# A hybrid encoder block on one core: gate row moved into gate/up, down-phase buffers and queue order rearranged

## The chip, the cores and the metric

One core of one Trainium2 chip runs the whole layer. The metric is the device time of one execution in microseconds (us); lower is better. TensorE (PE) does the matrix products, VectorE (DVE) and ScalarE (ACT) the elementwise work, GpSimd (POOL) a few copies and stores, and the sync engine (SP) issues nearly all transfers between device memory and the on-chip buffers, one after the other from one queue.

## The reference

The layer has three parts with a residual around each: a SwiGLU feed-forward network (FFN), a token mixer with two kinds of attention, and a second FFN. Each part is modulated from one condition vector c:

```
mod = silu(c) @ w_ada + b_ada            # 3 parts x (shift, scale, gate) x 1024
h = x + 0.5*g1 * postRMS(swiglu1(preRMS(x)*(1+scale)+shift))
h = h +     g2 * postRMS(mixer(...))
h = h + 0.5*g3 * postRMS(swiglu2(...))
swiglu(u) = (silu(u @ w_gate) * (u @ w_up)) @ w_down
```

There are 1024 tokens, a width of 1024 and a hidden width of 2816, all in 32-bit floats.

## The kernel before, in words

**Numbers.** Every operand of a product is split into a rounded high half (a cast on ScalarE, `ACT.copy`) and the remainder (a subtraction on VectorE). A product is three matmuls: high by high, high by low, low by high. So each loaded block costs one cast and one subtraction before TensorE can use it (`halves`, L218; `split`, L134).

**FFN, gate/up phase** (`ffn`, L498 to L556). The matrices are multiplied in 2x2 blocks by Winograd's scheme with seven block products in place of eight. Its operands of the token side are B11 and B21 (the plain halves, in U) and T1, T2, T3, T4 and B22, which `half1_blocks` puts into two pools on the left side of the buffer memory: T2, B22, T1 in one, T4 and T3 in the next. The 22 columns of 128 hidden features are taken as 11 pairs. For each pair there are two `Matrix` objects, gate and up, and `rest` (L414) runs the products of one: sums of its weight blocks on VectorE (`sums`, `sums34`, `last`), then p6 (with T2), p5 (T1), p7 (T3), p3 (B22), p4 (T4). After a pair, `hidden` (L458) forms the sums of the hidden blocks that the down phase needs and stores them to device memory; `down_sums` (L483) loads a pair's w_down blocks, forms the sums T1 to T4 of the down product and stores them too. For the pair with index 2 that call stands after the pair with index 4 (L551).

**FFN, down phase** (L558 to L641). Seven passes run over the 11 pairs, called blocks here, each pass with one operand s (a hidden block or sum) and one operand t (a weight block or sum), accumulating in one of two sets of four PSUM banks, A and B. Each block is loaded into a staging buffer `stg` (six of them), and split into `sb` (six) and `tb` (eleven) buffers. Passes 0 to 5 have 12 matmuls a block, the last pass runs in two halves with 6. Between passes the banks are copied or added into the rows y (L619 to L632): pass 3's banks B are copied by ScalarE and VectorE in turn, and pass 4 goes on accumulating in the same banks. `finish` (L583) loads the residual row, normalises, applies the gate row and stores.

**Modulation.** Generators make modulation vectors in small steps that are called between the blocks of other work: `mod_acc` (L82) loads eight 512 KB tiles of w_ada, one a step, and accumulates them on VectorE (L89, L91), with two empty steps after them. `mods` makes a shift and a scale, `mod_gate` (L114) a gate row: two matmuls (L125), two additions (L126), a product (L127), and a store (L130). `per_pair` says how many steps follow a pair in the gate/up phase, `STEPS` after which blocks one step is taken in each down pass. The first gate/up phase makes gate 0 and the mixer's shift and scale; the first down phase makes the mixer's gate and the second FFN's shift and scale; the second gate/up phase makes gate 2. The down phase loads the finished gate row (`grow`, L564) at its start.

**Mixer.** `mixer` (L749) begins with three projection jobs, whose four weight loads (L137, `Job.load`) stand at L1079.

**Order.** Each engine has one queue, worked in order. A scheduler lays it out when the kernel is built: by program order, but work whose operands and buffers are free is taken early, so loads and casts can stand far ahead of where the code has them. `tc.issue_after(ins)` forces everything traced inside it, on the engine of `ins`, behind `ins`. Pools opened in the same place of the memory follow each other, and a buffer can be written once the tiles that lay there are done.

Of the kernel before, what the change touches and what calls it, by code (L numbers as in the profile page):

```python
# [38 lines left out]
STEPS = ((0, 2, 4, 6, 8), (0, 2, 4, 6, 8), (2, 4, 6, 8, 10), (2, 6), (0, 4, 8), (4, 6, 8, 9, 10))  # L39
# [7 lines left out]
def build(ctx, tc, A, out):  # L47
# [84 lines left out]
    ab, gates = {}, {}  # L132

# [101 lines left out]
    def half1_blocks(pools, fp, psum, hn, abi, tag):  # L235


        a, b = abi

        def operands(pool, names):  # L240
            for n in names:
                TB[n] = [[pool.tile([P, HALF], F32R, name=f"{n}{hl}", tag=f"{n}{hl}", bufs=4) for _ in range(4)] for hl in "HL"]

        operands(pools[0], ("T2", "B22", "T1"))
        for q in range(4):
            V.tensor_sub(hn[q][:, :HALF], hn[4 + q][:, :HALF], hn[q][:, :HALF])

        def tile(n):
            return fp.tile([P, HALF], F32, name=n, tag="q", bufs=QT)

        def put(n, j, t):
            h, l = TB[n]
            h, l = h[j], l[j]
            ACT.copy(h, t)
            V.tensor_sub(l, t, h.bitcast(F32))

        def block(n, k, half, scale, bias, tag):
            t = tile(n)
# [12 lines left out]
        yield  # L271
        operands(pools[1], ("T4", "T3"))
        for j in range(4):
            put("B22", j, b22[j])
        for j in range(4):
            t3 = block("t3", j, 1, a[:, j:j + 1], b[:, j:j + 1], tag)
            V.tensor_sub(t3, b22[j], t3)
            put("T3", j, t3)
        for j in range(4):
            H21, L21 = (t.bitcast(F32) for t in U[j + 4, 0])  # L280
            V.tensor_sub(t2[j], H21, t2[j])
            V.tensor_add(t2[j], t2[j], L21)
            put("T4", j, t2[j])
        yield
# [129 lines left out]
    def rest(late, m):  # L414

        m.sums(late, False)
        m.sums34()
        m.last()
        m.p6()
        m.p5()  # L420
        m.p7()
        m.p3()
        m.p4()
# [74 lines left out]
    def ffn(wg, wu, wd, start, pending, steps_fn, per_pair, steps2_fn, i, res_src, dst):  # L498
# [4 lines left out]
        with tc.tile_pool(name="ffa", bufs=1, side="left", reuse_waits="tile") as fp, \  # L503
# [10 lines left out]
            with tc.tile_pool(name="fft", bufs=1, side="left", reuse_waits="tile") as tp, ExitStack() as more:  # L514
# [16 lines left out]
                with tc.tile_pool(name="late", bufs=1, side="right", reuse_waits="tile") as late:  # L531
                    steps = steps_fn(late, psum)
                    def follow(n):
                        if n % 2:
                            hidden(late, n // 2, mats[n // 2][1].c, hd)
                        if n > 1:
# [23 lines left out]
        with tc.tile_pool(name="ffb0", bufs=1, side="left", reuse_waits="tile") as np_, \  # L560
# [3 lines left out]
            SP.dma_start(grow, gates[i])  # L564
            steps = steps2_fn(np_, psum)
            B = {"B11": 0, "B21": 2, "B22": 3}

            def raw(n, c):
                t = fp.tile([P, HALF], F32, name="stg", tag="stg", bufs=STG)
                SP.dma_start(t, A[wd][c][:, B[n]] if n in B else hd[n, c])  # L570
# [7 lines left out]

            y = [y_tile(t) for t in range(NT)]
# [3 lines left out]
            def finish(t):  # L583
                res = np_.tile([P, D], F32, name="res", tag="res", bufs=2)
# [6 lines left out]
            for p, (sn, tn, bk) in enumerate((("A11", "B11", "A"), ("A12", "B21", "B"), ("S2", "T2", "A"), ("S1", "T1", "B"),  # L591
                                              ("S4", "B22", "B"), ("S3", "T3", "A"), ("A22", "T4", "A"))):
                if p in (0, 1, 3):
                    banks[bk] = [psum.tile([P, HALF], F32, name="bank" + bk, tag="p" + bk) for _ in range(4)]
                bank = banks[bk]
                fresh = p in (0, 1, 3)
                if p < 6:
                    for c in range(NPAIR):
                        s, t = halves(fp, raw(sn, c), "sb", SB), halves(fp, raw(tn, c), "tb", NPAIR)
# [4 lines left out]
                else:  # L604
                    ts = []
                    for h in range(2):
                        for c in range(NPAIR):
                            if h == 0 and c % 2 == 0:
                                next(steps, None)
                            r = raw(sn, c)  # L610
                            s = halves(fp, r[:, h * 256:(h + 1) * 256], "sb", SB, 256)
                            if h == 0:
                                ts.append(halves(fp, raw(tn, c), "tb", NPAIR))
                            for m in range(2):
                                mm(bank[2 * h + m], s, ts[c], slice(m * P, (m + 1) * P), False, c == NPAIR - 1, False)
                        for m in (2 * h, 2 * h + 1):
                            ACT.copy(y[4 + m][:, d0], bank[m])
                            finish(4 + m)
                for m in range(4):  # L619
# [6 lines left out]
                    elif p == 3:  # L626
                        (V.tensor_copy if m % 2 else ACT.copy)(y[4 + m][:, d1], bank[m])  # L627
# [3 lines left out]
                    elif p == 5:  # L631
                        V.tensor_add(y[4 + m][:, d1], bank[m], y[4 + m][:, d1])  # L632
# [107 lines left out]
    pending = ffn("wg1", "wu1", "wd1", start0, pending0, steps1, 3, steps1b, 0, lambda t: A["x"][t * P:(t + 1) * P, :], lambda t: h_dram[0][t])  # L740
# [3 lines left out]
    ffn("wg2", "wu2", "wd2", start_half, pending, lambda fp, psum: mod_gate(fp, psum, 2, 0.5), 1, no_steps, 2, lambda t: h_dram[1][t],  # L744
# [4 lines left out]
def mixer(e):  # L749
# [14 lines left out]
    with tc.tile_pool(name="mixa", bufs=1, side="left", reuse_waits="tile") as pa, \  # L764
# [314 lines left out]
        for job in first:  # L1079
            job.load()  # L1080
# [247 lines left out]
```

## Time and profile before

| what | value |
|---|---|
| runs | 2304.54, 2302.3, 2297.86 us; median 2302.3 |
| profiled execution | 2298.87 us, span 2297.1 us |
| TensorE busy | 2192.0 us, 95% of the span |
| VectorE busy | 1569.5 us, 68% |
| ScalarE busy | 1046.6 us, 46% |
| mean granted TensorE clock | 0.984 of 2.4 GHz |
| moved by transfers | 364.39 MB, mean 159 GB/s |

Busy time is the share in which an engine worked; a matmul's end is modelled, so idle time is read better from the starts. By lines and starts, the first gate/up phase runs to about 503 us, the first down phase to 748, the mixer and its merge to about 1630, the second gate/up phase to 2064, and the second down phase to the end.

### The profile page before, as it was taken

Reading aid. Unit: us, or ns where it says so; the run is one execution under the profiler, and the core shown is the slowest. Engines: PE = TensorE matmul, PEld = TensorE weight load, DVE = VectorE, ACT = ScalarE, POOL = GpSimd, SP = SyncE. Lnnn points to the kernel's source line nnn. Section 1 sums busy time; section 2 is a strip of 40 time slices with the busy share of each in tenths; the row PEclk is TensorE's granted clock in tenths of the full one; section 3 lists DMA queues with packets and bytes.
Section 4 is the critical chain, followed back from the end, with each engine's and each line's share of the span. In section 5 each row is a group of like instructions: output and inputs, shape, how many; then the busy total and the mean of one; then the engine's idle time right before and its main releaser. Section 6 shows DMA issues by size and latency. Waiting matters only on the chain.

```text
span 2297.1 us, 28628 instructions
## 1 busy us (share of the span) xinstructions
PE 2192.0 (95%) x10420; PEld 1796.2 (78%) x10420; DVE 1569.5 (68%) x2612; ACT 1046.6 (46%) x1882; POOL 70.2 (3%) x90
## 2 busy tenths in 40 slices
PE   5999999989989989999999999999999999999998
PEld 3787778868877877878888988788888788877886
DVE  6886686566767587576667577655895666655565
ACT  4633323235445465454545455554733333325454
POOL 1000000000000010011001010000000000000000
PEclk9999999999999999999999999999999999999999
DMA  7274665358877211110211122754474554427667
GB/s 303 87 266 161 226 233 187 127 197 297 298 241 241 68 42 40 42 49 25 66 56 58 44 94 74 238 195 133 152 249 167 179 174 142 169 101 259 209 208 245
DMA packets 137678, 364.39 MB, mean 159 GB/s; under 512 B 16704, under 2 KB 20800, under 8 KB 137536
## 3 DMA queue, kind: packets, MB, share of 16 engines
q1 hardware_dynamic: 135904, 356.79, 46.0%
q0 software_dynamic: 1632, 5.77, 0.6%
q8 instruction: 81, 1.33, 0.2%
q14 instruction: 61, 0.50, 0.1%
HBM read 272.32 MB, written 90.18 MB: 158 GB/s over the span
## 4 chain that ended last, share of the span: by engine, by line
PE 72%; DVE 15%; DMA 6%; ACT 4%; issue 2%; SPq 0%; DVEq 0%; ACTq 0%
PE bank L299 10%; PE bank L297 10%; PE bank L298 10%; PE pps L793 4%; PE pps L791 4%; PE pps L795 4%; PE bankA L575 3%; PE bankA L576 3%; PE bankA L577 3%; DVE f L988 2%; PE bankB L575 2%; PE bankB L576 2%; PE bankB L577 2%; DMA stg<-d_T 2%; PE vps L791 1%
## 5 line engine op out<-in xcount | busy, mean ns | idle before, releaser
L791 PE MATMUL pps<-uH,wsH 128*128 128x512 f32 x512 | 209.8, 410 | 0.0
L793 PE MATMUL pps<-uL,wsH 128*128 128x512 f32 x512 | 205.3, 401 | 0.0
L795 PE MATMUL pps<-uH,wsL 128*128 128x512 f32 x512 | 204.5, 399 | 0.0
L225 DVE TENSOR_TENSOR tbL<-stg,tbH 128x512 fp32r<-128x512 f32 x154 | 105.9, 690 | 113.2 <-ACT tbH L224 113.0
L224 ACT CAST tbH<-stg 128x512 fp32r<-128x512 f32 x154 | 95.5, 621 | 168.9 <-DMA stg<-d_T 100.3
L575 PE MATMUL bankA<-tbH,sbH 128*128 128x512 f32 x352 | 140.8, 402 | 17.8 <-ACT tbH L224 17.6
L297 PE MATMUL bank<-uH,wsH 128*128 128x512 f32 x352 | 140.6, 402 | 3.8 <-DVE uH L179 2.9
L298 PE MATMUL bank<-uL,wsH 128*128 128x512 f32 x352 | 140.0, 398 | 1.5 <-POOL uL L180 1.5
L576 PE MATMUL bankA<-tbL,sbH 128*128 128x512 f32 x352 | 140.3, 399 | 0.0
L577 PE MATMUL bankA<-tbH,sbL 128*128 128x512 f32 x352 | 139.5, 396 | 0.0
L299 PE MATMUL bank<-uH,wsL 128*128 128x512 f32 x352 | 138.9, 395 | 0.0
L141 DVE TENSOR_TENSOR wsL<-raw,wsH 128x1024 fp32r<-128x1024 f32 x72 | 87.9, 1221 | 69.6 <-ACT wsH L140 68.2
L225 DVE TENSOR_TENSOR sbL<-stg,sbH 128x512 fp32r<-128x512 f32 (+1 forms) x176 | 108.8, 620 | 33.8 <-ACT sbH L224 31.6
L224 ACT CAST sbH<-stg 128x512 fp32r<-128x512 f32 (+1 forms) x176 | 98.9, 565 | 62.8 <-DMA stg<-hd_A 32.4
L224 ACT CAST wsH<-s 128x1024 fp32r<-128x1024 f32 x88 | 91.7, 1050 | 64.8 <-DVE s L331 46.2
L364 ACT COPY q<-bank 128x512 f32<-128x512 f32 x44 | 25.8, 587 | 206.6 <-PE bank L299 206.6
L575 PE MATMUL bankB<-tbH,sbH 128*128 128x512 f32 x264 | 104.0, 394 | 7.5 <-ACT y L627 6.9
L795 PEld LDWEIGHTS pps<-uH,wsL 128*128 128x128 f32 x512 | 96.8, 189 | 17.9
L225 DVE TENSOR_TENSOR wsL<-s,wsH 128x1024 fp32r<-128x1024 f32 x88 | 107.0, 1218 | 5.3 <-ACT wsH L224 4.6
L791 PEld LDWEIGHTS pps<-uH,wsH 128*128 128x128 f32 x512 | 97.4, 190 | 14.8
L793 PEld LDWEIGHTS pps<-uL,wsH 128*128 128x128 f32 x512 | 97.2, 190 | 14.6
L224 ACT CAST wsH<-raw 128x1024 fp32r<-128x1024 f32 (+1 forms) x88 | 73.2, 834 | 75.2 <-PE bank L298 47.4
(247 smaller groups left out, 5957.9 us busy)
## 6 DMA issues: line engine op xcount, KB each, us to landing
wada<-in_wada SPq DMA_DIRECT2D x56, 512.0 KB, 5.3
raw<-in_wg SPq DMA_DIRECT2D x50, 512.0 KB, 6.1
raw<-in_wu SPq DMA_DIRECT2D x50, 512.0 KB, 4.5
raw<-in_wd SPq DMA_DIRECT2D x44, 512.0 KB, 4.3
stg<-hd_A SPq DMA_DIRECT2D x88, 256.0 KB, 4.3
stg<-d_S SPq DMA_DIRECT2D x88, 256.0 KB, 3.2
stg<-d_T SPq DMA_DIRECT2D x88, 256.0 KB, 3.5
d_S<-s SPq DMA_DIRECT2D x40, 512.0 KB, 2.7
```

Source lines behind the costliest of these rows:

```text
L141: eng.tensor_sub(l, raw, h.bitcast(F32))
L224: ACT.copy(h, src)
L225: V.tensor_sub(l, src, h.bitcast(F32))
L297: PE.matmul(ps, H[:, ks], bH, start=first and k == 0, stop=False, skip_group_check=not first)
L298: PE.matmul(ps, H[:, ks], bL, start=False, stop=False, skip_group_check=not first)
L299: PE.matmul(ps, L[:, ks], bH, start=False, stop=k == 3, skip_group_check=not first)
L575: PE.matmul(ps, sH[:, ts], tH, start=first, stop=False, skip_group_check=not check)
L576: PE.matmul(ps, sH[:, ts], tL, start=False, stop=False, skip_group_check=not check)
L577: PE.matmul(ps, sL[:, ts], tH, start=False, stop=last, skip_group_check=not check)
L791: PE.matmul(ps, aH, bH, start=i == 0, stop=False)
L793: PE.matmul(ps, aH, bL, start=False, stop=False)
L795: PE.matmul(ps, aL, bH, start=False, stop=i == n - 1)
```

## The change

- **Gate row.** The mixer's gate (`mod_gate(…, 1, 1.0)`) is made in the first gate/up phase and not in the first down phase. `per_pair` becomes a function of the pair: in the first FFN 2 steps for index 1, 5 for the others up to 9, none for 10; in the second 2 from index 2 on. `STEPS` is rewritten for the 20 steps that are left in the first down phase.
- **Operands.** The second pool of `half1_blocks` holds T3 and then T4. In the second FFN there are seven residual buffers and not two, which also moves the block buffers of the down phase.
- **Extra `down_sums`.** The call for pair 2 moves from after pair 4 into the gate matrix of pair 4, ahead of p6.
- **Gate row's load** in the down phase goes from the start to pass 2.
- **Order in the down phase.** The copies of pass 3 and the adds of pass 5 are kept in `copies`; the casts and subtractions of block 3 and later of passes 4 and 6 are traced behind them.
- **Mixer's loads.** The first three jobs' loads are traced behind the down phase's load number 110, the first of pass 5.

```diff
-STEPS = ((0, 2, 4, 6, 8), (0, 2, 4, 6, 8), (2, 4, 6, 8, 10), (2, 6), (0, 4, 8), (4, 6, 8, 9, 10))
+STEPS = ((6, 8, 10), (0, 3, 6, 9), (1, 3, 5, 7), (2, 6, 9), (2, 5, 8), (4, 6, 8))
-        operands(pools[1], ("T4", "T3"))
+        operands(pools[1], ("T3", "T4"))
@@ rest
         m.last()
+        if between is not None:
+            between()
         m.p6()
@@ ffn, gate/up
-                            for _ in range(per_pair // 2 + (n % 2) * (per_pair % 2)):
+                            for _ in range((per_pair(n // 2) + n % 2) // 2):
-                            rest(late, m)
+                            rest(late, m, None if second or c != NFIRST + 1 else
+                                 lambda: down_sums(fp, late, A[wd][NFIRST - 1], NFIRST - 1, hd))
-                        if c == NFIRST + 1:
-                            down_sums(fp, late, A[wd][NFIRST - 1], NFIRST - 1, hd)
-                        for _ in range(per_pair):
+                        for _ in range(per_pair(c)):
@@ ffn, down
-            SP.dma_start(grow, gates[i])
+            if i == 2:
+                res_bufs = 2 + 5
+            else:
+                res_bufs = 2
+                if p == 2:
+                    SP.dma_start(grow, gates[i])
+                        ahead = ExitStack()
+                        if p == 4 and c >= 3:
+                            for ins in copies:
+                                ahead.enter_context(tc.issue_after(ins))
+                        with ahead:
+                            s, t = halves(fp, raw(sn, c), "sb", SB), halves(fp, raw(tn, c), "tb", NPAIR)
...
-                            if h == 0 and c % 2 == 0:
+                            if h == 0 and c == 0:
                                 next(steps, None)
+                            with ExitStack() as ahead:
+                                if h == 0 and c >= 3:
+                                    for ins in copies:
+                                        ahead.enter_context(tc.issue_after(ins))
...
-                        (V.tensor_copy if m % 2 else ACT.copy)(y[4 + m][:, d1], bank[m])
+                        copies.append((V.tensor_copy if m % 2 else ACT.copy)(y[4 + m][:, d1], bank[m]).ins)
-                        V.tensor_add(y[4 + m][:, d1], bank[m], y[4 + m][:, d1])
+                        copies.append(V.tensor_add(y[4 + m][:, d1], bank[m], y[4 + m][:, d1]).ins)
@@ steps1, steps1b and the calls
         yield from mods(fp, psum, 1)
+        yield from mod_gate(fp, psum, 1, 1.0)
     def steps1b(fp, psum):
-        yield from mod_gate(fp, psum, 1, 1.0)
         yield from mods(fp, psum, 2)
-    ... steps1, 3, steps1b, ...
+    ... steps1, lambda c: 2 if c == 1 else 5 if c < 10 else 0, steps1b, ...
-    ... mod_gate(fp, psum, 2, 0.5), 1, no_steps, ...
+    ... mod_gate(fp, psum, 2, 0.5), lambda c: 2 if c > 1 else 0, no_steps, ...
@@ mixer
-        for job in first:
-            job.load()
+        with tc.issue_after(n.after[0][10 * NPAIR].ins):
+            for job in first:
+                job.load()
```

## Rows read from the trace of the kernel before

**Rows 1.** Windows: stretch, length, busy us (instructions) by engine, clock, transfer share, GB/s.
```profile
502.90:523.00 20.10, 11.90 (x30) 8.85 (x31) 12.26 (x19) 6.96 (x12) 1.20 (x3) 0.66 0.99 366
530.00:565.00 35.00, 35.00 (x157) 28.96 (x156) 23.73 (x33) 19.22 (x34) 0.00 (x0) 1.00 0.81 271
637.70:652.00 14.30, 6.82 (x21) 4.83 (x21) 10.42 (x15) 6.24 (x11) 0.00 (x0) 0.76 0.89 292
...
2063.60:2080.00 16.40, 6.98 (x19) 5.26 (x20) 8.47 (x13) 5.54 (x9) 0.94 (x2) 0.69 0.94 324
...
262.60:270.00 7.40, 4.82 (x15) 3.45 (x14) 6.68 (x10) 3.24 (x4) 0.00 (x0) 0.77 0.90 306
...
1830.00:1836.00 6.00, 4.61 (x19) 3.13 (x19) 4.79 (x7) 3.50 (x5) 0.00 (x0) 1.00 0.98 338
...
66.00:500.00 434.00, 427.68 (x1846) 342.76 (x1845) 317.71 (x434) 159.37 (x225) 2.31 (x4) 0.99 0.54 184
```

**Rows 2.** Timeline of TensorE: start, duration, line, operation, [idle before and its releaser].
```profile
508.15 0.79 PE L575 MATMUL bankA<-tbH,sbH 128*128 128x512 f32 x1 [5.27 <-ACT tbH L224]
...
515.97 1.65 PE L575 MATMUL bankA<-tbH,sbH 128*128 128x512 f32 x3 [2.95 <-ACT tbH L224]
...
644.68 0.80 PE L575 MATMUL bankB<-tbH,sbH 128*128 128x512 f32 x1 [6.85 <-ACT y L627]
...
2073.02 0.80 PE L575 MATMUL bankA<-tbH,sbH 128*128 128x512 f32 x1 [9.42 <-ACT tbH L224]
```

**Rows 3.** Timeline of the sync queue (SPq) at the start of the first down phase.
```profile
501.02 0.33 SPq L137 DMA_DIRECT2D raw<-in_win  x1
501.44 0.38 SPq L570 DMA_DIRECT2D stg<-hd_A  x1
```

**Rows 4.** Chain of waits in order of time: start, duration, what.
```profile
503.76 11.46 DMA stg<-in_wd
```

**Rows 5.** The line L570 (all block loads): time from issue to landing.
```profile
DMA to landing us min/median/max: 2.5/3.9/11.6
```

**Rows 6.** Timeline of the sync queue, second down phase.
```profile
2066.14 0.33 SPq L130 DMA_DIRECT2D g_dram<-grow  x1
2066.52 0.47 SPq L570 DMA_DIRECT2D stg<-hd_A  x1
...
2099.56 0.42 SPq L585 DMA_DIRECT2D res<-h_dram  x1
```

**Rows 7.** Timeline of ScalarE between passes 3 and 4 of the first FFN.
```profile
643.00 0.62 ACT L224 CAST tbH<-stg 128x512 fp32r<-128x512 f32 x1 [1.90 <-DMA stg<-in_wd]
...
644.05 0.58 ACT L627 COPY y<-bankB 128x512 f32<-128x512 f32 x1
```

**Rows 8.** Page, groups: line, engine, operation, shapes, count, busy us, mean ns, idle before.
```profile
L225 DVE TENSOR_TENSOR tbL<-stg,tbH 128x512 fp32r<-128x512 f32 x154 | 105.9, 690 | 113.2 <-ACT tbH L224 113.0
...
L141 DVE TENSOR_TENSOR wsL<-raw,wsH 128x1024 fp32r<-128x1024 f32 x72 | 87.9, 1221 | 69.6 <-ACT wsH L140 68.2
```

**Rows 9.** Timeline of VectorE after the fifth pair of the first FFN.
```profile
259.49 0.68 DVE L494 TENSOR_TENSOR t<-raw,t 128x512 f32<-128x512 f32 x1
260.09 1.27 DVE L126 TENSOR_TENSOR grow<-gps,br 128x512 f32<-128x512 f32 x2
...
261.89 1.21 DVE L127 SCALAR_TENSOR_TENSOR grow<-grow,npr 128x1024 f32<-128x1024 f32 x1
```

**Rows 10.** The line L91 (modulation sums): durations min/median/max ns, and waits before it.
```profile
L91 DVE SCALAR_TENSOR_TENSOR macc<-wada,csil,macc x49: 1273/1279/1286, 116.8 to 1712.0; 128x1024 f32<-128x1024 f32 x49
...
  DMA wada<-in_wada: 11.3, 8
```

**Rows 11.** Timelines at pass 6 of the second FFN: TensorE, VectorE, ScalarE.
```profile
2255.86 0.47 PE L575 MATMUL bankA<-tbH,sbH 128*128 128x512 f32 x1
...
2256.23 1.88 DVE L632 TENSOR_TENSOR y<-bankA,y 128x512 f32<-128x512 f32 x3
...
2268.05 0.41 ACT L224 CAST sbH<-stg 128x256 fp32r<-128x256 f32 x1
```

More of the change, by code (lines that the diff above doesn't have):

```diff
@@ L132, in build @@
     ab, gates = {}, {}
+    after = []
     def split(src, pool=None, tag="ws", bufs=4, eng=V):
@@ L412, in block_of, with rest @@
         return lambda k: (H[k], L[k])
-    def rest(late, m):
+    def rest(late, m, between=None):
         m.sums(late, False)
@@ L563, in ffn @@
             grow = np_.tile([P, D], F32, name="grow", tag="grow")
-            SP.dma_start(grow, gates[i])
+            if i == 2:
+                res_bufs = 2 + 5
+            else:
+                res_bufs = 2
             steps = steps2_fn(np_, psum)
             B = {"B11": 0, "B21": 2, "B22": 3}
+            loads = []
+            after[:] = [loads]
             def raw(n, c):
                 t = fp.tile([P, HALF], F32, name="stg", tag="stg", bufs=STG)
-                SP.dma_start(t, A[wd][c][:, B[n]] if n in B else hd[n, c])
+                loads.append(SP.dma_start(t, A[wd][c][:, B[n]] if n in B else hd[n, c]))
                 return t
@@ L577, in mm @@
                 PE.matmul(ps, sL[:, ts], tH, start=False, stop=last, skip_group_check=not check)
+            copies = []
             y = [y_tile(t) for t in range(NT)]
@@ L583, in finish @@
             def finish(t):
-                res = np_.tile([P, D], F32, name="res", tag="res", bufs=2)
+                res = np_.tile([P, D], F32, name="res", tag="res", bufs=res_bufs)
                 SP.dma_start(res, res_src(t))
@@ L598, in ffn @@
                     for c in range(NPAIR):
-                        s, t = halves(fp, raw(sn, c), "sb", SB), halves(fp, raw(tn, c), "tb", NPAIR)
+                        ahead = ExitStack()
[4 more added lines that the diff above has]
+                            s, t = halves(fp, raw(sn, c), "sb", SB), halves(fp, raw(tn, c), "tb", NPAIR)
                         if c in STEPS[p]:
@@ L607, in ffn @@
                         for c in range(NPAIR):
-                            if h == 0 and c % 2 == 0:
+                            if h == 0 and c == 0:
                                 next(steps, None)
[L610 to L613, printed above, removed]
+                            with ExitStack() as ahead:
+                                if h == 0 and c >= 3:
+                                    for ins in copies:
+                                        ahead.enter_context(tc.issue_after(ins))
+                                r = raw(sn, c)
+                                s = halves(fp, r[:, h * 256:(h + 1) * 256], "sb", SB, 256)
+                                if h == 0:
+                                    ts.append(halves(fp, raw(tn, c), "tb", NPAIR))
                             for m in range(2):
@@ L618, in ffn @@
                             finish(4 + m)
+                copies.clear()
                 for m in range(4):
@@ L738, in no_steps @@
         yield
-    pending = ffn("wg1", "wu1", "wd1", start0, pending0, steps1, 3, steps1b, 0, lambda t: A["x"][t * P:(t + 1) * P, :], lambda t: h_dram[0][t])
+    pending = ffn("wg1", "wu1", "wd1", start0, pending0, steps1, lambda c: 2 if c == 1 else 5 if c < 10 else 0, steps1b, 0, lambda t: A["x"][t * P:(t + 1) * P, :], lambda t: h_dram[0][t])
     pending = mixer(locals())
-    ffn("wg2", "wu2", "wd2", start_half, pending, lambda fp, psum: mod_gate(fp, psum, 2, 0.5), 1, no_steps, 2, lambda t: h_dram[1][t],
+    ffn("wg2", "wu2", "wd2", start_half, pending, lambda fp, psum: mod_gate(fp, psum, 2, 0.5), lambda c: 2 if c > 1 else 0, no_steps, 2, lambda t: h_dram[1][t],
         lambda t: out[t * P:(t + 1) * P, :])
```

## The prediction

> **What bounds the kernel now.** I read the page first: TensorE is busy nearly everywhere, so a change that keeps every product (this one does) can win only the time in which TensorE stands still or runs at the lower clock. I then listed TensorE's waits over the span, and laid windows around the long ones [rows 1]. The undisturbed stretch 530 to 565 has 157 matmuls in 35 us, 0.223 us each; the reader is to take each window's length less its matmuls times 0.223 as what was lost there, idle and slow clock together:
> - A, start of the first down phase: 20.1 - 30 x 0.223 = 13.4 us, granted clock 0.66, that is partly the 1.2 GHz level.
> - B, from pass 3 to pass 4 in that phase: 14.3 - 21 x 0.223 = 9.6.
> - C, after the fifth pair of the first gate/up phase: 7.4 - 15 x 0.223 = 4.1.
> - D, the same place in the second gate/up phase: 6.0 - 19 x 0.223 = 1.8.
> - E, start of the second down phase: 16.4 - 19 x 0.223 = 12.2.
>
> Together 41.1 us. Next the single waits: TensorE stood 5.27 and 2.95 us in A, 6.85 in B, 9.42 in E [rows 2]; and the queues that were late. In A the sync queue shows a mixer weight load at 501.02 and the first block load of the phase only behind it, at 501.44 [rows 3]; the block load issued at 503.76 landed 11.46 us later [rows 4], where the median is 3.9 [rows 5], and that is the 2.95. In E the store of the gate row (L130) goes at 2066.14 and the block loads stand behind it [rows 6]. In B ScalarE ran block casts that were waiting for transfers before the bank copy at 644.05, although the bank was complete at 644.68 - 6.85 = 637.83 [rows 2, 7].
>
> **The change part by part.** *A.* Three edits meet here. The mixer's first four loads are tied behind the first load of pass 5, the gate row's load goes to pass 2, and pass 0 takes its first modulation step at block 6 instead of 0, so the sync queue has block loads first. Swapping T3 and T4 puts the lowest tbL buffers, by my reading of the pool order, over T3, whose last use is a product earlier than T4's. The staging buffers lie over T2, dead four products of 12 matmuls, 48 x 0.223 = 11 us, before the phase ends, so six loads can land before TensorE needs them. Left over: casts and subtractions share VectorE (0.69 us each, [rows 8]) with the last pair's sums. Ends: 0 if all precede the last product, 13.4 if the queue order doesn't move. I take 1.5, since two subtractions of 0.69 stand before the first three products: gain 11.9.
>
> *B.* Casts from block 3 of pass 4 now stand behind the copies on ScalarE, and subtractions behind those on VectorE. A copy took 0.58 us and TensorE began 0.63 us after its start; with a short handover 0.9 stays (ends 0.6, and 9.6 if the casts of blocks 0 to 2 are late too): gain 8.7. The added wait holds eight blocks of casts. Three blocks already cast feed 3 x 12 x 0.223 = 8.0 us of products and three more wait in staging; the copies need two rounds of 0.6 us. So the cover is several times the wait. Pass 4 alone costs nothing; if the cover were gone, each lost block costs its load's 3.9.
>
> *E.* The gate steps run two a pair from the third pair on, so L127 and L130 end in the seventh or eighth pair, and nothing on the sync queue stands before the block loads. Seven residual buffers move the block buffers up 20 KB per partition, off the q tiles that live to the end, over the T operands. As in A, 1.0 stays (the copies of a gate row are absent here): gain 11.2, ends 0 and 12.2.
>
> *C and D.* In C VectorE ran four `down_sums` operations of 0.68 us for the third pair and three gate operations, 1.27 for two and 1.21, ahead of the sums that TensorE waited for [rows 9]. The extra `down_sums` goes ahead of p6 inside the fifth pair, where VectorE has slack. Gate 0 now ends after the fourth pair and the mixer's gate after the tenth, each with about 2.4 us of VectorE work at a boundary. TensorE lost 4.1 with 5.1 us of such work, so 2.4 alone costs between 0 and 4.1; nearest is D, 1.8 with 2.7 us. I take 1.0 for each gate: C gains 4.1 - 2.0 = 2.1. D loses its `down_sums` but gains a gate: 1.8 - 0.5 - 1.0 = 0.3.
>
> *The gate row itself.* Its 8 loads and 8 VectorE operations (49 of 1.28 us in the run, [rows 10]) go from the first down phase to the first gate/up phase, about 10 + 2.4 us onto VectorE, which there is busy 317.7 of 434 us [rows 1]; 330 of 434 still leaves it second to TensorE. But VectorE waited 11.3 us in 8 places on such loads [rows 10]; two or three more, of which TensorE feels some, cost 1.0 (ends 0 and 11). Its loads pass the sync queue among the weight loads; a wait there holds the next pair's weights, which are one product ahead. TensorE's own share only moves.
>
> *The mixer's loads later.* Four casts and four subtractions of 1.22 [rows 8] leave the end of gate/up, where they were free, for passes 4 to 6. Pass 4 has slack; if they fall into pass 5 with the normalisations they delay the transposes at its end. Below nothing is possible since modulation work left; I take 0.5 (ends -1.5 and 5).
>
> *Pass 6.* Here the added order holds only VectorE's subtractions, from block 3 on, behind the four adds of pass 5 (1.88 us for three, [rows 11]). In its first half a block feeds 6 x 0.223 = 1.34 us of products and needs 0.52 MB, which is 390 GB/s, above the 366 moved in A's window [rows 1]. Before, the last cast of this half was at 2268.05 [rows 11], just in time: its last block begins at 2255.9 + 10 x 1.34 = 2269.3. Holding blocks 3 and 4 some 2 to 3 us holds staging and so the loads of blocks 6 to 10, 2.6 MB or 7.2 us at 366. I take 1.5 in the first FFN and 0.5 in the second, 2.0 (ends -0.7, the wait now seen, and 2 x 5).
>
> *A rule against part E.* The load at 503.76 that landed 11.46 us later [rows 4] had larger loads before it. The Trainium skill's page DMA: Bandwidth & Descriptors, section Queues, rings and completion order, says that on each DMA engine descriptors are consumed in ring order, so a small load can't pass larger ones issued before it. The row agrees. By that rule seven residual loads hoisted to the phase's start would undo most of E's gain, where I charge none: it is a rival below, priced from rows.
>
> **Sum.** 11.9 + 8.7 + 11.2 + 2.1 + 0.3 = 34.2, less 1.0 + 0.5 + 2.0 gives 30.7 us. The profiled execution took 2298.9 us (span 2297.1 and 1.8 around it): 2268. It lies 3.4 below the median of the three runs, 2302.3, from which it would be 2272. I forecast 2270.
>
> **Rivals.**
> - *The starts stay late (gain 11 to 24).* The change does not do what it says there: other hoisted loads take the mixer loads' place. In E, five more residual buffers of 0.52 MB are 1.43 us each at 366 GB/s, 7.2 us ahead of blocks: 2277; with A unmoved too, 2289. For: the trace shows loads hoisted far. Against: before, two residual loads were issued only 26 us into that phase, the first at 2099.56 [rows 6], and the q tiles under the new ones live to the end of gate/up.
> - *The gate/up phases pay (gain 15 to 26).* Each of three gate endings costs the full 4.1 of C instead of 1.0, and the longer chain of modulation loads 4 instead of 1: 9.3 + 3 = 12.3 less, 2282. For: C; against: 5.1 us of work fell together there.
> - *Held splits starve TensorE: slower.* In passes 4 and 6 of both FFNs TensorE runs out of split blocks and each is a cold start like A. 4 x 13.4 = 53.6 us against 34.2 - 1.5 = 32.7 won: 2323. It decides from about 8 us in each of the four places. For: pass 6 needs more than the 366 GB/s. Against: six blocks are split or staged when the hold begins, in A none.
> - *All is won.* The residuals vanish: 41 us, 2260.
>
> **How the numbers follow.** The forecast's own case (gain 26 to 38, 2263 to 2276) has 0.55; gate/up pays 0.18; late starts 0.13; all won 0.07; no effect within 7 us 0.03; slower 0.04. 0.3%, about what a measurement of this kernel tells from no change, is 7 us. Faster 0.93, same 0.03, slower 0.04. The range 2259 to 2288 leaves out the slower case, the no-change case and the ends of the others.
>
> **What would show it.** Right: first matmul of each down phase under 2 us after the last gate/up product, granted clock 1.0 there; the L627 copies right after pass 3; no L137 load on the sync queue before pass 4; L130 twice in the first gate/up phase and once in the middle of the second. Wrong: TensorE gaps over 2 us at pair boundaries behind L126 and L127, or in the first half of pass 6 behind tbL; residual loads ahead of the first block loads. The forecast fails if A and E keep more than 10 us together, or if new waits of over 10 us come up in gate/up or pass 6.

## The result, and the profile after

| | before | after |
|---|---|---|
| median of the runs, us | 2303.03 (2297.86 to 2304.54, 4 runs) | 2283.39 (2280.65 to 2285.29, 4 runs) |
| span of the profiled execution, us | 2297.1 | 2278.7 |
| mean granted TensorE clock | 0.984 | 0.989 |

After takes 0.9916 of the time of before, 95% interval 0.9898 to 0.9935: 19.6 us less, where the sum of the prediction gave 30.7. The time lies inside the range 2259 to 2288, with a gain (19.6) that belongs to the rivals "starts stay late" (11 to 24) and "gate/up pays" (15 to 26), not to the forecast's own case (26 to 38).

The windows of after at the five places A to E (columns as in [rows 1]), and the stretch between passes 5 and 6 of the first FFN:

```profile
500.00:515.00 15.00, 12.06 (x53) 9.62 (x52) 10.40 (x17) 3.97 (x8) 1.61 (x3) 1.00 0.67 227
625.00:640.00 15.00, 14.88 (x65) 11.70 (x65) 12.11 (x20) 10.29 (x19) 0.00 (x0) 1.00 0.79 250
240.00:250.00 10.00, 7.99 (x33) 5.69 (x32) 7.94 (x10) 3.42 (x5) 0.00 (x0) 1.00 0.81 291
1788.00:1800.00 12.00, 9.55 (x35) 7.01 (x34) 5.64 (x7) 3.87 (x6) 0.00 (x0) 0.86 0.70 234
2050.00:2062.00 12.00, 9.07 (x40) 7.12 (x39) 8.68 (x14) 2.65 (x6) 1.61 (x3) 1.00 0.62 208
685.00:711.00 26.00, 20.31 (x96) 16.14 (x95) 23.38 (x47) 15.93 (x32) 0.00 (x0) 0.87 0.68 228
```

Length less matmuls times 0.223, as in the prediction: A lost 13.4 before and 3.2 now, B 9.6 and 0.5, C 4.1 and 2.6, D 1.8 and 4.2, E 12.2 and 3.1. That is 27.5 us won of 34.2 forecast. The last row is a place that the prediction had not listed as a loss. The same 26 us around the end of pass 5 read so before, 28 TensorE instructions more, at the full clock:

```profile
705.00:731.00 26.00, 23.17 (x124) 18.99 (x122) 22.04 (x45) 14.87 (x31) 0.00 (x0) 1.00 0.70 240
```

Transposes and matmuls mix there, so I added up by how much each distance between starts exceeds the median of its line: 3.5 us before, 10.1 after. So 6.6 us went there. In the second down phase behind E's window the same sum went from 0.7 to 2.4, another 1.6 us, and the mixer with its merge took 0.5 more. That brings 27.5 to 18.8; the span fell by 18.4. The second gate/up phase is 4.5 us longer by starts (438.7 to 443.2): 2.4 of that is D, and the rest is the gate row's own four matmuls, which before stood behind the phase's last product, ahead of E's window. That is work that moved, and no loss:

```profile
2061.72 1.88 PE L125 MATMUL gps<-macc,ones 128*128 128x512 f32 x4
```

TensorE's waits in after (start, duration, line, operation, [idle before and its releaser]), the answer to [rows 2]:

```profile
245.14 0.50 PE L298 MATMUL bank<-T2H,wsH 128*128 128x512 f32 x1 [1.60 <-ACT wsH L225]
...
506.33 0.50 PE L584 MATMUL bankA<-tbL,sbH 128*128 128x512 f32 x1 [2.94 <-DVE tbL L226]
...
692.62 2.25 PE L187 MATMUL tps<-ident,y 128*128 128x128 f32 x10 [3.61 <-DVE y L172]
...
698.55 0.66 PE L187 MATMUL tps<-ident,y 128*128 128x128 f32 x4 [1.62 <-DVE y L172]
...
1794.47 0.50 PE L298 MATMUL bank<-uH,wsH 128*128 128x512 f32 x1 [2.45 <-ACT wsH L225]
```

The 5.27, 6.85 and 9.42 are gone. In A the releaser is no longer a cast that waits for a load but a subtraction. The transposes (L187) wait twice for normalised rows (L172), and the first wait was followed by a stretch at 0.5 of the clock, the 1.2 GHz level (692.8 to 696.2). The 3.61 is new; a wait like the second stood there before as well:

```profile
712.53 0.66 PE L186 MATMUL tps<-ident,y 128*128 128x128 f32 x4 [1.65 <-DVE y L171]
```

What stands ahead of the first subtractions in A now is VectorE's own order at that place:

```profile
503.06 0.68 DVE L468 TENSOR_TENSOR s<-s,q 128x512 f32<-128x512 f32 x1
503.67 0.68 DVE L355 TENSOR_TENSOR q<-bank,q 128x512 f32<-128x512 f32 x1
504.38 0.69 DVE L470 TENSOR_TENSOR s<-q,s 128x512 f32<-128x512 f32 x1
504.99 0.68 DVE L226 TENSOR_TENSOR sbL<-stg,sbH 128x512 fp32r<-128x512 f32 x1
505.59 0.68 DVE L226 TENSOR_TENSOR tbL<-stg,tbH 128x512 fp32r<-128x512 f32 x1
```

and it isn't the loads: on the sync queue the phase's first block load stands at 489.90, the first mixer load (L138 in after) only at 642.88, where [rows 3] had the mixer's load first:

```profile
489.90 0.33 SPq L578 DMA_DIRECT2D stg<-hd_A  x1
...
493.88 0.38 SPq L578 DMA_DIRECT2D stg<-in_wd  x1
505.70 0.33 SPq L578 DMA_DIRECT2D stg<-hd_A  x1
...
642.88 0.43 SPq L138 DMA_DIRECT2D raw<-in_win  x1
```

Six loads by 494, then none until a subtraction frees a staging buffer. E looks the same (first block load 2039.57, against 2066.52 in [rows 6], and 2.9 us of idle).

Part of this is luck. The same wait of 2.94 us stands at both starts in ten traces of this kernel and its variants (after, e1 to e3, e5, e6, e8 to e10, e12). Where the granted clock stayed at 1.00 behind it, the start lost 3.3 us; where it fell to 0.5, 4.8 to 6.2. In after it fell at neither start, in each of the other nine at one or both. And after's profiled execution is the fastest of its four, with a mean clock of 0.989 where the other three have 0.985 and 0.986. So A and E are read here at their best, and a difference of up to some 3 us between after and another run can be this alone.

In D the sync queue again shows the cause:

```profile
1781.14 6.38 SPq L484 DMA_DIRECT2D d_T<-t  x4
1787.57 0.46 SPq L316 DMA_DIRECT2D raw<-in_wu  x1
```

Four stores of the extra `down_sums`, now ahead of p6 in the fifth pair, take the queue from 1781.1 to 1787.5, since each waits for its sum on VectorE (the last at 1786.32), and the next matrix' weights are issued behind them; they reach ScalarE's cast at 1793.37, and TensorE stands until 1794.47.

### The profile page after: what moved, and what is told of

Its sections match the earlier page's. It is cut to its first block, busy times and chain, and to the rows that moved or that the text cites. A ratio compares the mean times of both kernels' runs of the same rounds, so it can differ in the third digit from the quotient of the medians.

```text
span 2278.7 us, 28622 instructions
## 1 busy us (share of the span) xinstructions
PE 2189.4 (96%) x10420; PEld 1792.8 (79%) x10420; DVE 1566.4 (69%) x2612; ACT 1043.7 (46%) x1882; POOL 70.0 (3%) x90
## 4 chain that ended last, share of the span: by engine, by line
PE 66%; DVE 17%; DMA 10%; ACT 5%; issue 2%; SPq 0%; DVEq 0%; ACTq 0%
PE bank L300 9%; PE bank L298 9%; PE bank L299 9%; PE pps L815 4%; PE pps L813 4%; DMA stg<-d_T 4%; PE pps L817 4%; DVE f L1010 2%; PE bankA L585 2%; PE bankA L584 2%; PE bankA L583 2%; DMA wada<-in_wada 2%; PE vps L813 1%; PE vps L817 1%; PE vps L815 1%
## 5 line engine op out<-in xcount | busy, mean ns | idle before, releaser
L142 DVE TENSOR_TENSOR wsL<-raw,wsH 128x1024 fp32r<-128x1024 f32 x72 | 88.0, 1222 | 70.4 <-ACT wsH L141 69.0
```

What stands on the lines that cost most here:

```text
L142: eng.tensor_sub(l, raw, h.bitcast(F32))
```

## The experiments

Each kernel is the changed one with the edit shown. e1 to e11 ran once each, so I read them by the stage that the edit touches; between single executions the whole time differs by some 5 us (after's runs lie 4.6 apart). "Loss before pass 6" is the sum over distances named above.

**e1, the mixer's loads one and a half passes earlier.**
```diff
-        with tc.issue_after(n.after[0][10 * NPAIR].ins):
+        with tc.issue_after(n.after[0][6 * NPAIR].ins):
```


> The changed kernel, with one edit: the mixer's first loads stand behind the first block load of pass 3 and not of pass 5. In the changed kernel the mixer's subtractions (1.22 us each, one waiting for its load) stand on VectorE ahead of the adds after pass 4, and TensorE then loses about 10 us at the transposes before pass 6 (3.61 and 1.62 idle, the rest slow clock), against 3.5 before. Theory 1, the mixer's loads made that: the adds follow pass 4 within 1 us, and the loss falls to 2 to 5 us, time 5 to 8 us less than the changed kernel's 2279 (profiled span), so 2271 to 2274. Theory 2, the subtractions held behind the adds of pass 5 made it: the loss stays at 8 to 11 us and the span at 2277 to 2281.

2287.7 us. The loss before pass 6 stayed at 10.6, and the mixer's casts and subtractions now stood ahead of the copies between passes 3 and 4 (4 us there). The first down phase took 236.4 us, 230.9 in after. So in this place the mixer's loads alone don't make the loss before pass 6. The adds of pass 4 (L651) were just as late, behind other work on VectorE, and this time with no mixer operation near:

```profile
667.62 0.69 DVE L226 TENSOR_TENSOR tbL<-stg,tbH 128x512 fp32r<-128x512 f32 x1 [1.46 <-ACT tbH L225]
668.23 0.68 DVE L226 TENSOR_TENSOR sbL<-stg,sbH 128x512 fp32r<-128x512 f32 x1
668.83 2.48 DVE L651 TENSOR_TENSOR y<-bankB,y 128x512 f32<-128x512 f32 x4
```

**e2, no hold of pass 6.**
```diff
-                        copies.append(V.tensor_add(y[4 + m][:, d1], bank[m], y[4 + m][:, d1]).ins)
+                        V.tensor_add(y[4 + m][:, d1], bank[m], y[4 + m][:, d1])
```


> The changed kernel without the order of pass 6: the subtractions of its blocks from 3 on are no longer held behind the adds of pass 5. Theory 1 (the mixer's loads): the loss before pass 6 of the first FFN stays at 8 to 11 us, the second FFN's pass 6 changes by less than 1.5 us, span 2276 to 2281. Theory 2 (the held subtractions): the loss falls to about 4 us and the span to 2271 to 2274.

2290.3 us. The loss before pass 6 rose to 12.2 in the first FFN, and in the second a wait came up at the same place where after has none:

```profile
2246.29 0.77 PE L583 MATMUL bankA<-tbH,sbH 128*128 128x512 f32 x1 [4.51 <-DVE y L654]
```

The second down phase took 220.7 us, 214.8 in after; 1.6 of the difference is the lower clock at its start, and around the wait shown 6.2 us were lost where after lost 0.8. The hold of pass 6, which I charged with 2.0, gains some 5 us in the second FFN and 2 in the first: pass 6 goes on in bank A and can't start before pass 5's adds (L654) have read it.

**e3, T4 ahead of T3 again**, and **e4, two residual buffers in the second FFN.**
```diff
-        operands(pools[1], ("T3", "T4"))
+        operands(pools[1], ("T4", "T3"))
```


> The changed kernel with T4 allocated below T3 again, as before the change. The instruction order on every engine is the same, only addresses and waits differ. Theory 1, the order of VectorE decides at the start of the down phases (the last pair's sums ahead of the first subtractions, 2.9 us of idle TensorE): no difference, idle 2.5 to 3.5 us in both starts, span within 2 us of 2279. Theory 2, the swap is worth something by itself: the first tbL waits for the last product p4, which ends about 4 us before that subtraction runs in the changed kernel; if other waits follow it, each start grows by 1 to 4 us and the span is 2281 to 2287.

```diff
-                res_bufs = 2 + 5
+                res_bufs = 2
```


> The changed kernel with two residual buffers in the second FFN, so that its block buffers lie 20 KB lower, over hidden tiles (q) that live to the end of the gate/up phase. Theory 1, the early gate row alone freed the sync queue and that was the whole of the 12.2 us lost at the second down start: idle stays near 3 us, span within 2 us of 2279. Theory 2, the buffers' place was the other half: the staging loads wait until the hidden tiles' stores are done, land some 4 us later, and the start loses 6 to 10 us again with a drop of the granted clock, span 2283 to 2287.

e3: 2282.6 us, the idle at both starts as in after (2.94 each); the swap is worth nothing that can be seen. e4: 2293.5 us; its second down phase began at 2065.1 and not at 2052.9, with its first block load on the sync queue at 2060.73 instead of 2039.57:

```profile
2065.09 0.79 PE L583 MATMUL bankA<-tbH,sbH 128*128 128x512 f32 x1 [9.11 <-ACT tbH L225]
```

An early gate row with the buffers in their old place leaves E as it was (9.42 in [rows 2]). So E needs the block buffers where they now lie, off the tiles that live to the phase's end; no store stood ahead of the loads in e4 (the gate row's went at 1941.3). Whether the early gate row was needed beside that isn't shown: the new place with a late gate row wasn't run.

**e5, the hold on pass 5 too**, so that its splits stand behind pass 4's adds.
```diff
-                        if p == 4 and c >= 3:
+                        if p in (4, 5) and c >= 3:
...
-                        V.tensor_add(y[m][:, d1], bank[m], y[m][:, d1])
+                        copies.append(V.tensor_add(y[m][:, d1], bank[m], y[m][:, d1]).ins)
```


> The changed kernel with one more hold: casts and subtractions of pass 5 from block 3 on stand behind pass 4's four adds, as those of pass 4 and 6 do already. Theory 3 (the 10.1 us that the changed kernel loses between passes 5 and 6 of the first FFN come from pass 4's adds standing on VectorE behind subtractions of pass 5 that wait for loads: the first add began 3.9 us after pass 4's end, 1.1 before the change): the first add begins under 1.5 us after pass 4's end, the loss before pass 6 falls from 10 to about 6, time 2279 to 2281. Rival (the four rows' normalisation takes its 34 to 36 us wherever it begins, and pass 5's blocks are held without cover): the loss before pass 6 stays over 9, gaps of over 1 us appear in pass 5, time 2284 to 2290.

2285.1 us, loss before pass 6 10.0, adds 4.1 us after pass 4's end (3.9 in after). My theory fell in this form; the row ahead of the adds says why:

```profile
655.58 0.68 DVE L226 TENSOR_TENSOR sbL<-stg,sbH 128x512 fp32r<-128x512 f32 x1
660.57 2.47 DVE L142 TENSOR_TENSOR wsL<-raw,wsH 128x1024 fp32r<-128x1024 f32 x2 [4.31 <-ACT wsH L141]
662.96 2.48 DVE L651 TENSOR_TENSOR y<-bankB,y 128x512 f32<-128x512 f32 x4
```

With the blocks' subtractions held, the mixer's (L142), waiting 4.31 us for casts that wait for their own loads, stand there instead. That suggests two waits side by side, each hiding the other; e9 tries it.

**e6, the transposes behind pass 6's first half.**
```diff
                         for m in (2 * h, 2 * h + 1):
                             ACT.copy(y[4 + m][:, d0], bank[m])
                             finish(4 + m)
+                        if h == 0 and i + 1 in ab:
+                            list(transpose_half(np_, psum, y, 0, ab[i + 1], tag="pB", mtag="u32"))
...
-                if p == 5 and i + 1 in ab:
-                    list(transpose_half(np_, psum, y, 0, ab[i + 1], tag="pB", mtag="u32"))
```


> The changed kernel with the first half's transposes (L187) put behind the first half of pass 6 instead of ahead of it. Nothing is left out. Theory 3 says that TensorE stands before pass 6 only because of the normalised rows: with 8 blocks of 6 products between, about 11 us, the rows are ready, the loss before pass 6 falls from 10.1 to under 3 and the time to 2275 to 2278. Rival (pass 6's own splits are just as late, since its first half needs a block each 1.34 us): the loss moves into the first half of pass 6, and the time stays at 2281 to 2287.

2291.7 us. My theory missed: the loss moved into pass 6's first half, as the rival said, but the time is above the rival's range too, and the wait isn't the one that it named. Without transposes TensorE stood at the same place, now not for splits but for pass 5's adds, which on VectorE came after the normalisation, and 4.6 us more at 727 for a block's subtraction.

```profile
697.83 0.77 PE L583 MATMUL bankA<-tbH,sbH 128*128 128x512 f32 x1 [5.37 <-DVE y L656]
```

**e7, the last pair's four hidden sums on GpSimd.**
```diff
+        E = POOL if c == NPAIR - 1 else V
-        V.tensor_add(s21[:, 1], a21, a22)
+        E.tensor_add(s21[:, 1], a21, a22)
...
```
(The three subtractions likewise.)


> The changed kernel with the four sums of hidden tiles of each phase's last pair (L467 to L470) on GpSimd instead of VectorE. Theory 1 (the 2.9 us that TensorE still stands at the start of each down phase is VectorE's queue: five sums of 0.68 us ahead of the first subtractions): both gaps fall under 1 us, 4 to 5 us less in all, time 2278 to 2280. Rival (the sums on GpSimd are slower, and the last pair's own stores or casts behind them become late): gaps at the start stay over 2 us or gaps come up within passes 2 and 3, time 2283 to 2290.

2281.2 us, but the wait at the starts grew, to 3.4 us in the first phase. VectorE and GpSimd there (start, duration, line, operation):

```profile
503.66 0.69 DVE L355 TENSOR_TENSOR q<-bank,q 128x512 f32<-128x512 f32 x1 [1.38 <-PE bank L300]
504.27 1.30 DVE L226 TENSOR_TENSOR sbL<-stg,sbH 128x512 fp32r<-128x512 f32 x1
505.49 1.75 DVE L226 TENSOR_TENSOR tbL<-stg,tbH 128x512 fp32r<-128x512 f32 x1
507.16 2.25 DVE L226 TENSOR_TENSOR sbL<-stg,sbH 128x512 fp32r<-128x512 f32 x1
```
```profile
503.76 1.26 POOL L470 TENSOR_TENSOR s<-q 128x512 f32<-128x512 f32 x1
504.99 1.70 POOL L469 TENSOR_TENSOR s<-s,q 128x512 f32<-128x512 f32 x1
...
507.57 1.29 POOL L471 TENSOR_TENSOR s<-q,s 128x512 f32<-128x512 f32 x1
```

The first subtraction still stands behind the last product (L355), which waits for TensorE's last bank. And each subtraction now ends 0.55 us after a GpSimd operation ends (505.02 and 505.57, 506.69 and 507.24, 508.86 and 509.41). The Trainium skill's page SBUF — State Buffer, section SBUF: two separate sides, says that VectorE with two SBUF inputs and GpSimd share one pair of ports by an exclusive lock, so that one blocks fully; these rows agree.

**e8, the extra `down_sums`' stores on GpSimd's queue.**
```diff
-                                 lambda: down_sums(fp, late, A[wd][NFIRST - 1], NFIRST - 1, hd))
+                                 lambda: down_sums(fp, late, A[wd][NFIRST - 1], NFIRST - 1, hd, POOL))
```
(`down_sums` and `both` take the queue as an argument.)

> The changed kernel with the four stores of the extra down sums (L484, for the third pair) issued from GpSimd's queue instead of the sync queue. Theory (in C and D the sync queue stands on these stores, 6.38 us for four in the second phase, with the next weight loads behind them): those loads are issued 5 us earlier, the loss in D falls from 4.45 to about 1.5 and in C from 2.8 to about 1.5, time 2279 to 2281. Rival (the sums themselves, on VectorE ahead of p6's operations, make the loss): C and D as in the changed kernel within 0.7 us, time 2282 to 2286.

2278.8 us. The load that stood at 1787.57 goes at 1782.42, the second gate/up phase takes 439.8 us (443.2 in after, 438.7 before), and D's wait is 1.0 (2.6 in after, by distances between starts). C didn't get better (3.0 where after has 1.8, both above the spacing of the matmuls): there three modulation loads (L87) hold the queue from 236.1 to 241.9, ahead of the next weights.

**e9, both waits ahead of pass 4's adds away:** e5's edit, and the mixer's loads in the second half of pass 6.
```diff
-        with tc.issue_after(n.after[0][10 * NPAIR].ins):
+        with tc.issue_after(n.after[0][14 * NPAIR].ins):
```


> The changed kernel with both things taken away that stood on VectorE ahead of pass 4's adds: the hold of e5 on pass 5, and the mixer's first four loads behind the first load of the second half of pass 6. In e1 the adds stood behind block subtractions, in e5 behind the mixer's subtractions (L142), 3.8 and 4.1 us after pass 4's end each time. Theory 3 in its second form (two waits side by side, each covering the other): the first add begins under 1.5 us after pass 4's end, the loss before pass 6 falls from 10 to about 6, the mixer's start costs under 2 us, time 2278 to 2281. Rival (the loss comes from the order behind the adds, where rows' stores stand on the sync queue ahead of block loads): adds early, loss before pass 6 still over 9, time 2282 to 2288.

2281.5 us. Now nothing but TensorE's bank is ahead of the adds, and the stretch before pass 6 has 34 TensorE instructions more than in after and stays at the full clock:

```profile
660.96 2.73 DVE L651 TENSOR_TENSOR y<-bankB,y 128x512 f32<-128x512 f32 x4 [2.15 <-PE bankB L585]
```
```profile
685.00:711.00 26.00, 24.45 (x130) 20.01 (x129) 23.37 (x49) 17.02 (x35) 0.00 (x0) 1.00 0.72 239
```

The loss before pass 6 is 3.4, about what it was before the change (3.5); the first down phase takes 226.0 us, the mixer with its merge 874.8 (875.6 in after), so its later loads cost nothing. This goes beyond the 6 that I expected. In the second FFN, where the mixer has no part, 4.0 us went in pass 5 (a wait of 2.1 at 2220.8 and a lower clock behind it). I put that down to the hold, but e5 has the same hold there and lost 0.6 in the same stretch, so one run can't charge it. With it, and with both starts followed by the lower clock (6.2 and 4.9 lost, 3.3 each in after), the whole time gained little. The later loads without the hold weren't run. That both edits are needed is argued, from e5, which has the hold alone, and from e1, where the mixer's loads are gone from this place but disturb passes 3 and 4.

**e10, the stores of finished rows on GpSimd's queue.**
```diff
-            SP.dma_start(dst[:, c], y[:, c])
+            (q or SP).dma_start(dst[:, c], y[:, c])
```
(q is GpSimd in the first FFN's `finish`.)

> The changed kernel with the eight stores of finished rows (L217) of the first FFN on GpSimd's queue instead of the sync queue. In the changed kernel the sync queue waits 5.1 us in three places for such rows, with loads of blocks behind (the next blocks of pass 6 are issued at 697.3, 8 us after pass 5's end). Theory 4 (that queue keeps both pass 6's blocks and, over VectorE's order, the normalisation late): loss before pass 6 falls from 10 to 3 to 6, time 2276 to 2280. Rival, theory 3: the adds still begin 3.9 us late and VectorE's order is the same, so the loss stays at 9 to 11, time 2282 to 2286.

2304.7 us, the worst of all: both theories missed. The span is 24 us longer than after's: 11.6 in the first down phase, 6.0 in the mixer, and 4.0 in the first gate/up phase, which the edit doesn't touch; the last two stay unexplained. Scaling a row in place (L172) has to wait until its store has read it, and from this queue that takes longer: 5.7 us median from issue to landing for 512 KB against 3.7 for the same eight stores in after.

```profile
684.82 0.75 DVE L172 TENSOR_SCALAR y<-y,rs 128x1024 f32<-128x1024 f32 x1 [3.36 <-DMA h_dram<-y]
...
695.83 0.75 DVE L172 TENSOR_SCALAR y<-y,rs 128x1024 f32<-128x1024 f32 x1 [1.82 <-DMA h_dram<-y]
```

Whether the sync queue's waits for rows cost anything by themselves stays open: this run moved them and lengthened them at once. What it does show is that TensorE waits when the rows' chain is late (8.9 us at the transposes behind 696.6).

**e11, e8 and the last product too on GpSimd** (ScalarE copies its bank).
```diff
+                if self.tail and n == "C21":
+                    x = self.q()
+                    ACT.copy(x, src)
+                    POOL.tensor_mul(t, x, t)
...
```


> e8 (stores of the extra down sums on GpSimd's queue) and, in each phase's last pair, the last product (L355 after a copy of its bank by ScalarE) and the four sums on GpSimd. In e7 the first subtractions still stood behind that product on VectorE, which waits for the bank's last matmul, and then took 1.3 to 2.3 us each beside GpSimd's sums. Theory (the place in VectorE's order, not the number of sums): first subtractions begin before the last product's end and the gap at each start falls from 2.9 to under 1 us; with e8's gain 2272 to 2275. Rival (VectorE, at half its pace beside GpSimd, is what TensorE waits for): gaps stay over 2 us, time 2277 to 2281.

2284.3 us. The wait moved to ScalarE: its copy, waiting 7.8 us for the bank, stands ahead of the casts, and TensorE waits 1.7 and 1.5 us at each start (1.71 and 1.55 in the second). So the traces of after, e7 and e11 all have the last pair's work ahead of the first splits in an in-order queue, but no run shortened the wait at A and E, and that this order is its cause isn't shown; an order that puts the first subtractions ahead of the last product wasn't tried.

**e12, what helped, together:** e8, e9's later mixer loads, and the hold on pass 5 in the first FFN alone.

> The changed kernel with three edits: the hold on pass 5 in the first FFN alone, the mixer's first four loads behind pass 6's first half (both as in e9), and the stores of the extra down sums on GpSimd's queue (e8). e9's first down phase was 4.9 us shorter than the changed kernel's (226.0 against 230.9), e8's second gate/up phase 3.4 us shorter (439.8 against 443.2), and e9's loss of 4 us in pass 5 of the second FFN goes with the hold there. If the three add up: 4.9 + 3.4 = 8 us less than 2283.4, that is 2275 (2272 to 2279), ratio to the kernel before 0.986 to 0.990. Rival (the later start of one phase changes which transfers meet, and single profiles differ by as much): 2279 to 2285, ratio 0.990 to 0.992.

2273.6 us (2271.95 to 2275.37, 4 runs; before beside it 2303.32), ratio 0.9872, interval 0.9856 to 0.9889, which lies below after's 0.9898 to 0.9935: faster than both kernels, by about 10 us than after. The first down phase takes 224.2 us, the second gate/up phase 439.7, the loss before pass 6 is 2.9, D's window is nearly full:

```profile
685.00:711.00 26.00, 24.59 (x131) 19.94 (x129) 22.14 (x46) 15.44 (x32) 0.00 (x0) 1.00 0.75 237
1784.00:1802.00 18.00, 17.75 (x77) 14.15 (x77) 10.71 (x14) 7.71 (x11) 0.00 (x0) 1.00 0.56 206
```

A and E have the idle of after (2.9 us each), but here both were followed by the lower clock, and each start lost 4.9 us.

## Why the prediction was right and where it was wrong

The time lies inside the range, but the sum is 11 us off, and two of its terms have the wrong sign. A, B and E came as argued, A and E less some. The gain falls where two rivals have it, but neither names what cost most, the end of pass 5; that the range holds even so is luck, and not a mechanism that was foreseen.

- **A and E, right in kind, 3.8 us short.** 10.2 and 9.1 won for 11.9 and 11.2. Queue order and buffers did what I said (loads some 13 us ahead of each phase; e4 for the buffers). What was left, 1.5 and 1.0, was priced as two subtractions; 3.2 and 3.1 are left. In the trace the subtractions stand behind the last pair's sums and its last product; that this order is the cause isn't shown (e7 and e11 moved the wait and didn't shorten it). And 3.2 and 3.1 are the lucky end: with the lower clock behind the wait it is 4.9. The swap of T3 and T4, which I gave a part in A, has none that shows (e3).
- **The rule against E** (ring order, residual loads ahead of blocks): the first block load went at 2039.57, before the phase, with the gate row's store at 1938.42. The rival fell. The page of the Trainium skill that the prediction names there orders how descriptors are consumed; that a small load can't pass a larger one is the prediction's own step. The trace bears it out here: in before no transfer of the sync queue landed ahead of one issued before it (958 transfers).
- **B, right.** 9.1 for 8.7; the copies went at 627.63 on ScalarE.
- **C, near: 1.5 for 2.1. D, wrong in sign: 2.4 lost for 0.3 won.** I counted the moved `down_sums` as VectorE's work with slack, and left out that its four stores take their place on the sync queue, where each waits for a sum with the next weights behind it (e8: 3.4 us of the phase).
- **Gate row, right.** VectorE was to be busy about 330 us of the first gate/up phase and is 327; TensorE's idle time there didn't grow: 437 less 431.4 is 5.6 us by the row below, 6.3 in [rows 1], and outside C's windows 3.6 and 3.7. Of the 1.0 charged nothing shows.

```profile
66.00:503.00 437.00, 431.40 (x1870) 345.00 (x1869) 327.31 (x446) 159.31 (x228) 2.31 (x4) 1.00 0.56 195
```

- **Mixer's loads later: the step that failed.** I took 0.5, with ends of -1.5 and 5, and named the way ("they delay the transposes at its end"). The loss was 6.6, outside the ends. My cover, "pass 4 has slack", was counted in VectorE's busy time, and what counts is who stands ahead of pass 4's adds in VectorE's queue. Before, block subtractions did; after, a mixer subtraction that waits for its cast, and block subtractions behind it (first before, then after):

```profile
677.25 0.69 DVE L225 TENSOR_TENSOR tbL<-stg,tbH 128x512 fp32r<-128x512 f32 x1 [2.51 <-ACT tbH L224]
...
678.46 2.48 DVE L629 TENSOR_TENSOR y<-bankB,y 128x512 f32<-128x512 f32 x4
```
```profile
659.47 1.23 DVE L142 TENSOR_TENSOR wsL<-raw,wsH 128x1024 fp32r<-128x1024 f32 x1 [1.65 <-ACT wsH L141]
660.62 0.68 DVE L226 TENSOR_TENSOR tbL<-stg,tbH 128x512 fp32r<-128x512 f32 x1
662.00 0.69 DVE L226 TENSOR_TENSOR tbL<-stg,tbH 128x512 fp32r<-128x512 f32 x1 [0.70 <-ACT tbH L225]
662.61 2.48 DVE L651 TENSOR_TENSOR y<-bankB,y 128x512 f32<-128x512 f32 x4
```

  With the adds begins the chain that normalises four rows, and the transposes need its end. By starts, three things made it late against TensorE. The first add came 4.1 us after pass 4's last matmul began (658.49), 1.3 before (677.18). From there to the end of the last row the chain took 35.9 us, 34.0 before. And from pass 4's last matmul to pass 5's TensorE took 29.9 us, 31.8 before, because 16 modulation matmuls (L101) that stood there at 688.3 to 690.1 moved elsewhere: a gain on TensorE that the chain turned into waiting, and that my argument leaves out. The three add up to the 6.6. In e9 TensorE took 29.9 us too, and the chain 37.7, but the first add came 1.6 us before pass 4's last matmul began, and only 3.4 was lost: the loss hangs on what stands ahead of the adds. There block work hid the mixer's wait, and the mixer's the blocks' (e1, e5).
- **Pass 6's hold, wrong in sign.** Charged with 2.0; it gains some 7 (e2). I looked at the bandwidth that pass 6 needs and not at the bank: it can't start before pass 5's adds.

Terms: 27.5 of the 34.2 came; of the 3.5 in costs, the hold was a gain already inside the trace of after, and pass 5's end took 6.6 for 0.5.

## What to carry to other kernels

An operation that waits at the head of an in-order queue costs whatever stands behind it, however idle the engine: when work is moved, list its loads, stores, casts and subtractions on every queue that they join, and who is next there. Before forecasting a gain at the start of a stage, follow the longest chain that runs beside it (here rows' normalisation beside pass 5), since that becomes the bound when the stage starts earlier. Where one removal changes nothing, look for a second wait in the same place before dropping the theory.

## What the runs showed of the hardware that I had not expected

- Subtractions of 128x512 on VectorE took 1.30 to 2.25 us beside GpSimd's elementwise operations, 0.68 without them (e7).
- The first FFN's eight 512 KB stores landed 5.7 us after issue from GpSimd's queue (median; 2.9 to 7.0, e10), 3.7 from the sync queue (after). The Trainium skill's page SBUF — State Buffer, section SBUF: two separate sides, says that VectorE operations can keep GpSimd from writing a transfer's descriptors. Here that can't be the whole cause: the store issued at 748.66 took 5.0 us, in which VectorE was busy for 0.16. The transfers' share was 0.85 then, and 0.45 around the two stores that took 2.9.
- Waits of the same length are not always followed by a lower clock: 2.94 us at the start of the first down phase left the granted clock at 1.00 in after, and the same 2.94 us in e3 was followed by 3.4 us at 0.5. Of 21 such waits at the starts of down phases (e4 has one, the ten traces named above two each), 13 were followed by 0.5.
